# A hybrid encoder trunk: the correction of a softmax's 1/sum written into the sum's PSUM bank, and another order of matmuls in the values' projection

## The chip, the cores and the metric

One core of a Trainium2 chip. The metric is the device time of one execution in microseconds (us), the median over several executions. The engines are PE (TensorE, with its weight loads, PEld), DVE (VectorE), ACT (ScalarE), POOL (GpSimd) and SP (SyncE, which issues the DMAs).

## The reference, cut to what matters

x is 1 x 1024 tokens x 1024 features, float32. Two layers, each with a mixer and a feed-forward part: layer 0 mixes with 8 heads of latent attention (MLA) and 8 heads of stick-breaking attention, layer 1 with 16 heads of attention in chunks over a band of 9 chunks of 64 tokens.

```python
# MLA, per block of 128 queries
p_a = jax.nn.softmax(jnp.where(chunk_ok, s_a, -jnp.inf), axis=-1)
outs_a.append(jnp.einsum('bhqk,bkhd->bqhd', p_a.astype(v_a.dtype), v_a[:, :kend]))
# band
p = jax.nn.softmax(jnp.where(valid[None, :, None, None, :], scores, -jnp.inf), axis=-1).astype(v.dtype)
parts = [jnp.einsum('bnhqk,bnkhd->bnqhd', p[..., i * CHUNK:(i + 1) * CHUNK], v_p[:, i:i + n_chunks])
         for i in range(LEFT_CHUNKS + 1)]
o = functools.reduce(jnp.add, parts)
```

In both softmaxes the kernel divides at the end: it sums the exponentials, multiplies the unnormalised result with 1/sum, and so needs one reciprocal of a 128 x 512 tile for each pair of heads and each half of the tokens.

## The kernel before, in words

Activations lie transposed, 128 features (or two heads of 64) on the partitions and 512 tokens (a half, `hf`) along the free dimension. A float32 product is made of three matmuls in the rounded type fp32r: high by high, high by low, low by high (`mm3`, L277 to L282, so a product shows as L280, L281, L282). A tile and its rest are made by `split`: a cast (L243 on ACT, or L245 on DVE and POOL) and a subtraction (L248, "rest").

A framework's scheduler orders the instructions of each engine by priority and its own cost estimates, gives out the buffers of each named pool and sets the semaphores; only the feed-forward parts keep the order of the program. PSUM has three pools: `mm` (2 buffers of one bank, `bank`), for projections; `z` (2 buffers of two banks, `banks`, L199), for scores, maxima and sums; `o` (2 banks), for attention results. The SBUF tiles named `f` rotate through 3 buffers in mixer 0 and 2 in mixer 1.

Attention runs head pair by head pair, and in each the first half of the tokens before the second. `weave` (L785) mixes its steps with a filling generator: the projections of the next head pair, and at their end the values of a coming one. For the softmaxes each step has score matmuls (L1120 to L1122 in MLA, L1201 and L1202 in the band) into a `z` buffer, an addition of the bias on DVE in the band (L1203), an exponential on ACT, the running sum `esum` on POOL (L1072), and the product with the values (L831). A second set of score matmuls (L1049 in MLA, L1175 in the band) and reductions on DVE (L1051, L1178, result `m`) find the maxima for the coming half.

`soft_finish` (L1084) ends each half of a head pair; it runs 8 times in MLA and 16 times in the band. Two matmuls for each of the two heads add up `esum` over the partitions into `den`, one bank of a `z` buffer (L1088). ACT forms r = exp(-ln(den)) (L1090, L1091). DVE then corrects r by one Newton step: t = -den * r (L1092), r = (t + 2) * r (L1093); and L1094 forms the result from `o`, a PSUM bank, and r.

`values` (L798) projects the values of two head pairs, 256 columns. Four tiles of weights, quarters with two of the 8 features each, are loaded and split (`wh` by ACT, `wl` by DVE; four buffers of each, shared with the other projections). The stationary operand is a block of 128 tokens, the moving one 128 x 256 weights, so that one bank of 512 columns takes two token blocks; a call for one half fills two banks. It is called in the stick-breaking part for head pairs 0 and 1, ahead of the band's attention, and in the band for head pairs 0 to 5. Calls for MLA's own values have one block in a bank.

## Time and profile before

| | us |
|---|---|
| median of 3 executions | 2609.49 |
| lowest, highest | 2604.78, 2610.32 |
| the profiled execution | 2615.43 |
| its span in the profile | 2613.3 |

The stages in the profiled execution, with busy time of PE and DVE in us and the mean granted clock of PE:

| stage | from, to | PE | DVE | POOL | clock |
|---|---|---|---|---|---|
| opening: norm, first values and keys | 0, 70 | 53.3 | 45.0 | 24.0 | 0.95 |
| stick-breaking attention, MLA's projections | 70, 430 | 342.2 | 308.9 | 128.8 | 0.99 |
| MLA's attention | 430, 660 | 223.6 | 158.0 | 120.6 | 0.98 |
| feed-forward 0 | 660, 1310 | 639.7 | 469.1 | 7.2 | 1.00 |
| band: first values and projections | 1310, 1376 | 63.1 | 40.8 | 16.7 | 1.00 |
| band's attention | 1376, 1905 | 516.3 | 384.5 | 194.5 | 1.00 |
| feed-forward 1 | 1905, 2550 | 635.6 | 466.7 | 4.4 | 0.99 |
| final norm | 2550, 2613 | 47.8 | 38.6 | 26.6 | 0.93 |

A row of the timeline gives start and duration of one instruction, its engine, line, operation and tiles (out<-in), and in brackets how long the engine stood idle before it and which instruction's semaphore ended that. PE's durations overlap, since matmuls are pipelined; the step from start to start is the rate. Rows of groups give count, busy time, mean duration in ns and the idle time before the group's instructions. The releaser of a wait is inferred.

### The profile page before, as it was taken

What the parts mean: (1) busy time and instruction counts of PE and PEld (TensorE: products, weight loads), DVE (VectorE), ACT (ScalarE), POOL (GpSimd) and SP (SyncE); (2) the same over time, 40 slices, a digit from 0 to 9 for tenths busy, and PEclk for the clock granted to TensorE, in tenths of its full rate; (3) what the DMA queues carried; (4) which work ended last, traced back from release to release, by engine and by line L of the source; (5) the groups of instructions that cost most, each with busy time, mean ns of one, the idle gap of its engine ahead of it and who ended that gap; (6) DMA issues with size and microseconds to landing.
All of it is one profiled execution on the core that took longest, in us unless ns stands there. A gap on an engine that the chain in (4) does not pass through costs nothing.

```text
span 2613.3 us, 33627 instructions
## 1 busy us (share of the span) xinstructions
PE 2521.6 (96%) x11758; PEld 1941.0 (74%) x11758; DVE 1911.5 (73%) x3072; ACT 1169.0 (45%) x2028; POOL 522.9 (20%) x489
## 2 busy tenths in 40 slices
PE   7999999999999999999999999999999999999997
PEld 6766765557778888888787666676777888888876
DVE  6888887775787666777666777777778766667776
ACT  4677676454454334432253333334444443443324
POOL 3333324663000000000021333335400000000004
PEclk9999998999999999999999999999999999999999
DMA  4221100125434344476642222222552434447661
GB/s 137 61 63 53 53 17 29 35 64 159 163 99 161 110 140 142 149 258 216 206 160 67 73 78 80 73 69 89 172 166 96 162 109 141 145 140 260 213 213 69
DMA packets 179433, 319.70 MB, mean 122 GB/s; under 512 B 20545, under 2 KB 36801, under 8 KB 179265
## 3 DMA queue, kind: packets, MB, share of 16 engines
q1 hardware_dynamic: 179264, 317.56, 36.8%
q8 instruction: 93, 1.52, 0.3%
q14 instruction: 76, 0.61, 0.1%
HBM read 222.58 MB, written 84.41 MB: 117 GB/s over the span
## 4 chain that ended last, share of the span: by engine, by line
PE 68%; DVE 12%; DMA 2%; issue 2%; ACT 2%; SPq 0%; DVEq 0%; ACTq 0%
PE z L74 24%; PE mm L74 12%; PE o L74 6%; PE mm L280 5%; PE mm L281 5%; PE mm L282 5%; PE o L831 3%; DVE u L74 2%; DVE f L1093 2%; PE z L1201 1%; PE z L1175 1%; PE z L1202 1%; DVE u L303 1%; DMA wr<-in_w_down 1%; PE z L1088 1%
## 5 line engine op out<-in xcount | busy, mean ns | idle before, releaser
L74 PE MATMUL z<-u,vh 128*128 128x512 f32 x976 | 304.6, 393 | 7.2 <-DVE u L74 7.2
L74 PE MATMUL z<-u,wh 128*128 128x512 f32 x976 | 302.3, 390 | 6.5 <-DVE u L74 6.5
L280 PE MATMUL mm<-u,wh 128*128 128x512 f32 x720 | 291.7, 405 | 2.4 <-DVE u L710 1.1
L281 PE MATMUL mm<-u,wh 128*128 128x512 f32 x720 | 284.4, 395 | 1.4 <-DVE u L248 1.4
L248 POOL TENSOR_TENSOR wl<-wr,wh 128x512 fp32r<-128x512 f32 (+2 forms) x95 | 123.6, 1308 | 802.4 <-ACT wh L243 733.6
L282 PE MATMUL mm<-u,wl 128*128 128x512 f32 x720 | 283.8, 394 | 0.0
L74 PE MATMUL mm<-u,wh 128*128 128x512 f32 x720 | 224.6, 393 | 3.8 <-ACT wh L74 3.8
L74 PEld LDWEIGHTS z<-u,vh 128*128 128x128 f32 x976 | 184.5, 189 | 48.1 <-ACT u L74 8.8
L74 PEld LDWEIGHTS z<-u,wh 128*128 128x128 f32 x976 | 183.1, 188 | 47.4 <-DVE u L74 9.4
L74 PE MATMUL z<-u,vl 128*128 128x512 f32 x488 | 191.1, 392 | 0.0
L74 PE MATMUL z<-u,wl 128*128 128x512 f32 x488 | 190.0, 389 | 0.0
L280 PEld LDWEIGHTS mm<-u,wh 128*128 128x128 f32 x720 | 135.6, 188 | 62.2 <-issue 33.1
L831 PE MATMUL o<-a,u 128*64 128x512 f32 (+3 forms) x768 | 172.4, 485 | 0.3 <-ACT a L1204 0.3
L74 PEld LDWEIGHTS mm<-u,wh 128*128 128x128 f32 x720 | 135.5, 189 | 34.9 <-ACT wh L74 5.7
L281 PEld LDWEIGHTS mm<-u,wh 128*128 128x128 f32 x720 | 135.8, 189 | 32.5 <-issue 8.3
L282 PEld LDWEIGHTS mm<-u,wl 128*128 128x128 f32 x720 | 135.5, 188 | 32.3 <-issue 3.6
L74 PE MATMUL mm<-u,vh 128*128 128x512 f32 x496 | 152.7, 389 | 0.0
L248 POOL TENSOR_TENSOR u<-wr,u 128x512 fp32r<-128x512 f32 x8 | 10.9, 1373 | 671.7 <-ACT u L243 671.7
L74 PE MATMUL mm<-u,wl 128*128 128x512 f32 x360 | 141.2, 392 | 0.7 <-DVE wl L74 0.5
L1204 ACT ACTIVATE a<-a 128x1024 f32<-128x1024 f32 (+3 forms) x96 | 70.6, 738 | 155.3 <-DVE a L1203 155.0
L1072 POOL TENSOR_TENSOR b<-b,a 128x512 f32<-128x512 f32 (+3 forms) x80 | 110.6, 1382 | 135.8 <-ACT a L1204 117.4
L1203 DVE TENSOR_TENSOR a<-z,bias 128x1024 f32<-128x1024 f32 (+3 forms) x96 | 78.7, 823 | 79.5 <-PE z L1202 65.6
(248 smaller groups left out, 5983.1 us busy)
## 6 DMA issues: line engine op xcount, KB each, us to landing
u<-f_t SPq DMA_DIRECT2D x144, 256.0 KB, 5.2
vr<-in_w_up SPq DMA_DIRECT2D x88, 256.0 KB, 4.4
wr<-in_w_gate SPq DMA_DIRECT2D x88, 256.0 KB, 3.5
f_t<-x SPq DMA_DIRECT2D x72, 256.0 KB, 2.0
wr<-in_w_out SPq DMA_DIRECT2D x64, 256.0 KB, 3.0
f_t<-e SPq DMA_DIRECT2D x54, 256.0 KB, 3.6
ld<-f SPq DMA_DIRECT2D x54, 256.0 KB, 5.2
h<-u SPq DMA_DIRECT2D x48, 256.0 KB, 2.5
```

The source lines that it names most:

```text
L74: return lambda *a, **k: self.tc.keep_in_program_order(f(*a, **k))
L248: self.eng(eng).tensor_tensor(lo, src, hi.bitcast(F32), ALU.subtract)
L280: mm(out, wh, xh, start=first, stop=False, skip_group_check=onto)
L281: mm(out, wh, xl, start=False, stop=False, skip_group_check=onto)
L282: mm(out, wl, xh, start=False, stop=last, skip_group_check=onto)
L303: self.eng(eng).tensor_tensor(acc, acc, sq, ALU.add)
L831: self.nc.tensor.matmul(o[rh, cs], vt[j // 4][:, j % 4, rh], w[:, e, cs], start=first, stop=last)
L1072: self.eng("dve" if dest[2] else "pool").tensor_tensor(st["esum"][:, :, cs], old[:, :, cs], ex[:, :, cs], ALU.add)
L1088: nc.tensor.matmul(den[64 * e:64 * e + 64, :], self.ones[:, 0:64], esum[:, e, :], start=True, stop=True)
L1093: nc.vector.scalar_tensor_tensor(r, t, 2.0, r, ALU.add, ALU.mult)
L1203: nc.vector.tensor_tensor(ex[:, :, cs], z[:, :, cs], tk[:, :, xs], ALU.add)
L1204: nc.scalar.activation(ex[:, :, cs], ex[:, :, cs], AF.Exp)
```

## The change

In `soft_finish` the tile t is gone: L1092 writes -den * r over den in its PSUM bank, and L1093 reads that bank and r. The `z` buffer that holds den is in use until L1093 now. In `values` the two loops are exchanged: for each feature k the three matmuls of the first block, then the three of the second; the first matmul of the bank alone clears it (start), and the last one ends it.

```diff
-            for b in range(per):
-                hf, r = divmod(b0 + b, 4)
-                ts = slice(r * P, (r + 1) * P)
-                for k in range(nk):
+            for k in range(nk):
+                for b in range(per):
+                    hf, r = divmod(b0 + b, 4)
+                    ts = slice(r * P, (r + 1) * P)
                     wh, wl = ws[k // kper].at(k % kper * ncol, ncol)
                     self.mm3(ps[:, b * ncol:(b + 1) * ncol], u[hf][0][k][:, ts], u[hf][1][k][:, ts],
-                             wh, wl, k == 0, k == nk - 1)
+                             wh, wl, k == 0 and b == 0, k == nk - 1 and b == per - 1)
                     yield 3 * MM_US * ncol / HALF
...
-        r, t, ot = self.tmp("f"), self.tmp("f"), self.tmp("f")
+        r, ot = self.tmp("f"), self.tmp("f")
         nc.scalar.activation(r, den, AF.Ln)
         nc.scalar.activation(r, r, AF.Exp, scale=-1.0)
-        nc.vector.scalar_tensor_tensor(t, den, -1.0, r, ALU.mult, ALU.mult)
-        nc.vector.scalar_tensor_tensor(r, t, 2.0, r, ALU.add, ALU.mult)
+        nc.vector.scalar_tensor_tensor(den, den, -1.0, r, ALU.mult, ALU.mult)
+        nc.vector.scalar_tensor_tensor(r, den, 2.0, r, ALU.add, ALU.mult)
```

The scheduler keeps the feed-forward parts as they were. Names carry running numbers, which are smaller after the change since a tile is missing.

DVE at the end of the band's first head pair, second half (f are r, t and ot, z den or scores, bias the bias, mm a projection). Before:

```order
L1203 TENSOR_TENSOR a_12987<-z_12988,bias_12786 128x2x384
L1092 SCALAR_TENSOR_TENSOR f_12979<-z_12975,f_12978 128x512
L1139 SCALAR_TENSOR_TENSOR t_13012<-mm_12951,u_11665 128x512
L1093 SCALAR_TENSOR_TENSOR f_12978<-f_12979,f_12978 128x512
L1178 ISA z_12999,m_12998<-z_12999,bias_12781 128x512
L1178 ISA m_12998 128x1
L1094 TENSOR_TENSOR f_12980<-o_12669,f_12978 128x512
L1178 ISA z_12999,m_12998<-z_12999,bias_12781 128x512
```

And after the change:

```order
L1203 TENSOR_TENSOR a_12977<-z_12978,bias_12777 128x2x384
L1092 SCALAR_TENSOR_TENSOR z_12966<-z_12966,f_12969 128x512
L1139 SCALAR_TENSOR_TENSOR t_13002<-mm_12942,u_11657 128x512
L1093 SCALAR_TENSOR_TENSOR f_12969<-z_12966,f_12969 128x512
L1178 ISA z_12989,m_12988<-z_12989,bias_12772 128x512
L1178 ISA m_12988 128x1
L1094 TENSOR_TENSOR f_12970<-o_12660,f_12969 128x512
L1178 ISA z_12989,m_12988<-z_12989,bias_12772 128x512
```

The order of DVE is the same there; den's buffer (z_12975, now z_12966) is read two instructions later than before.

PE at the same place, behind the sum's matmuls (L1088): score matmuls for the maxima (L1175) between those of a projection (L280 to L282). Before:

```order
L282 MATMUL mm_13024<-u_11698,wl_12942 128x512
L1175 MATMUL z_12999<-u_12641,u_12568 128x512
L1175 MATMUL z_12999<-u_12647,u_12573 128x512
L1175 MATMUL z_13004<-u_12692,u_12568 128x128
L1175 MATMUL z_13004<-u_12698,u_12573 128x128
L280 MATMUL mm_13024<-u_11725,wh_12941 128x512
L281 MATMUL mm_13024<-u_11726,wh_12941 128x512
```

After:

```order
L282 MATMUL mm_13014<-u_11690,wl_12933 128x512
L1175 MATMUL z_12989<-u_12632,u_12560 128x512
L1175 MATMUL z_12989<-u_12638,u_12565 128x512
L280 MATMUL mm_13014<-u_11717,wh_12932 128x512
L281 MATMUL mm_13014<-u_11718,wh_12932 128x512
L282 MATMUL mm_13014<-u_11717,wl_12933 128x512
L280 MATMUL mm_13014<-u_11745,wh_12932 128x512
L281 MATMUL mm_13014<-u_11746,wh_12932 128x512
L282 MATMUL mm_13014<-u_11745,wl_12933 128x512
L1175 MATMUL z_12994<-u_12683,u_12560 128x128
L1175 MATMUL z_12994<-u_12689,u_12565 128x128
```

The second pair of L1175 (z_13004, now z_12994) stands six matmuls of the projection later.

PE in the values' projection of the same head pair's first half (mm is the bank, wh and wl weights, u activations), around the first use of the fourth quarter of the weights (wh_12724 and wl_12725, now wh_12715 and wl_12716). Before, where the bank's first matmul stands 23 rows ahead of that use:

```order
L280 MATMUL mm_12728<-wh_12718,u_11597 128x256
L281 MATMUL mm_12728<-wl_12719,u_11597 128x256
L282 MATMUL mm_12728<-wh_12718,u_11598 128x256
L280 MATMUL mm_12728<-wh_12724,u_11625 128x256
L281 MATMUL mm_12728<-wl_12725,u_11625 128x256
L282 MATMUL mm_12728<-wh_12724,u_11626 128x256
```

After, where it stands 48 rows ahead:

```order
L280 MATMUL mm_12719<-wh_12709,u_11589 128x256
L281 MATMUL mm_12719<-wl_12710,u_11589 128x256
L282 MATMUL mm_12719<-wh_12709,u_11590 128x256
L280 MATMUL mm_12719<-wh_12715,u_11617 128x256
L281 MATMUL mm_12719<-wl_12716,u_11617 128x256
L282 MATMUL mm_12719<-wh_12715,u_11618 128x256
```

Of these rows 18 were matmuls of the values and are 36 now; the others are attention.

DVE in the stick-breaking attention of the first head pair, where the next projection's weights are cast (L245, wh) and their rests formed (L248, wl), between the steps of the attention (L897, L900, L924, L927). Before:

```order
L897 TENSOR_SCALAR a_1334<-z_1329 128x1024
L924 TENSOR_TENSOR b_999<-z_1318,b_999 1x1024
L900 TENSOR_TENSOR b_1269<-b_1269,a_1268 128x1024
L927 TENSOR_TENSOR a_1170<-a_1170,z_1318 128x1024
L248 TENSOR_TENSOR c_1275<-b_1269,c_1274 128x512
L900 TENSOR_TENSOR b_1335<-b_1335,a_1334 128x1024
L245 CAST wh_1417<-wr_1415 128x512
L245 CAST wh_1423<-wr_1421 128x512
L248 TENSOR_TENSOR wl_1418<-wr_1415,wh_1417 128x512
```

After:

```order
L245 CAST wh_1417<-wr_1415 128x512
L248 TENSOR_TENSOR wl_1418<-wr_1415,wh_1417 128x512
L897 TENSOR_SCALAR a_1334<-z_1329 128x1024
L924 TENSOR_TENSOR b_999<-z_1318,b_999 1x1024
L900 TENSOR_TENSOR b_1269<-b_1269,a_1268 128x1024
L927 TENSOR_TENSOR a_1170<-a_1170,z_1318 128x1024
L248 TENSOR_TENSOR c_1275<-b_1269,c_1274 128x512
L900 TENSOR_TENSOR b_1335<-b_1335,a_1334 128x1024
L245 CAST wh_1423<-wr_1421 128x512
```

The first cast and its rest stand ahead of L897 and six more instructions now.

## Rows read from the trace of the kernel before

**Rows 1.** The page: busy time, and the chain that ended last, by line.
```profile
PE 2521.6 (96%) x11758; PEld 1941.0 (74%) x11758; DVE 1911.5 (73%) x3072; ACT 1169.0 (45%) x2028; POOL 522.9 (20%) x489
...
PE z L74 24%; PE mm L74 12%; PE o L74 6%; PE mm L280 5%; PE mm L281 5%; PE mm L282 5%; PE o L831 3%; DVE u L74 2%; DVE f L1093 2%; PE z L1201 1%; PE z L1175 1%; PE z L1202 1%; DVE u L303 1%; DMA wr<-in_w_down 1%; PE z L1088 1%
```

**Rows 2.** Groups of DVE by line: count | busy us, mean ns | idle.
```profile
L1093 DVE SCALAR_TENSOR_TENSOR f<-f,f 128x512 f32<-128x512 f32 x24 | 45.0, 1877 | 0.6
```

**Rows 3.** Timeline of DVE and POOL, end of a first half in the band.
```profile
1436.95 2.83 DVE L1093 SCALAR_TENSOR_TENSOR f<-f,f 128x512 f32<-128x512 f32 x1
1439.81 0.69 DVE L248 TENSOR_TENSOR u<-t,u 64x512 fp32r<-64x512 f32 x1
...
1436.85 2.38 POOL L1072 TENSOR_TENSOR b<-a,a 128x1024 f32<-128x1024 f32 x1 [3.75 <-ACT a L1204]
```

**Rows 4.** Timeline of DVE, POOL and PE, end of a second half in the band.
```profile
1473.87 2.30 DVE L1093 SCALAR_TENSOR_TENSOR f<-f,f 128x512 f32<-128x512 f32 x1
1476.10 0.68 DVE L1178 CUSTOM_DVE_ANT_0 z<-z,bias 128x512 f32<-128x512 f32 x1
...
1473.78 1.84 POOL L1072 TENSOR_TENSOR b<-a,a 128x768 f32<-128x768 f32 x1 [5.99 <-ACT a L1204]
...
1478.10 0.39 PE L1201 MATMUL z<-u,u 128*128 128x256 f32 x1 [1.14 <-DVE m L1178]
```

**Rows 5.** Groups of PE by line, 1376 to 1905 us, idle time in the last column.
```profile
L1201 PE MATMUL z<-u,u 128*128 128x512 f32 (+3 forms) x192 | 66.4, 357 | 5.7 <-DVE m L1178 5.7
L281 PE MATMUL mm<-wl,u 128*128 128x256 f32 x202 | 57.7, 286 | 4.3 <-DVE wl L248 4.3
```

**Rows 6.** Timeline of PE and DVE, values' projection in a first half.
```profile
1445.27 0.28 PE L282 MATMUL mm<-wh,u 128*128 128x256 f32 x1
1445.38 0.28 PE L280 MATMUL mm<-wh,u 128*128 128x256 f32 x1
1446.15 0.39 PE L281 MATMUL mm<-wl,u 128*128 128x256 f32 x1 [0.49 <-DVE wl L248]
...
1444.10 2.00 DVE L248 TENSOR_TENSOR wl<-wr,wh 128x512 fp32r<-128x512 f32 x1 [0.82 <-ACT wh L243]
```

**Rows 7.** Timeline of PE, two starts of a projection in stick-breaking attention.
```profile
139.23 0.27 PE L895 MATMUL z<-u,u 128*128 128x128 f32 x1
140.03 0.51 PE L280 MATMUL mm<-u,wh 128*128 128x512 f32 x1 [0.53 <-DVE wh L245]
...
213.00 0.50 PE L280 MATMUL mm<-u,wh 128*128 128x512 f32 x1 [0.53 <-DVE wh L245]
```

**Rows 8.** Timeline of DVE, POOL and PE, a softmax's end in MLA.
```profile
511.60 0.69 DVE L1092 SCALAR_TENSOR_TENSOR f<-z,f 128x512 f32<-128x512 f32 x1
512.33 4.13 DVE L1093 SCALAR_TENSOR_TENSOR f<-f,f 128x512 f32<-128x512 f32 x1
...
510.99 1.18 POOL L248 TENSOR_TENSOR wl<-wr,wh 128x256 fp32r<-128x256 f32 x1
...
513.55 5.13 POOL L1072 TENSOR_TENSOR b<-b,a 128x1024 f32<-128x1024 f32 x2
...
517.57 0.44 PE L1120 MATMUL z<-u,u 104*128 104x384 f32 x1 [2.37 <-DVE m L1051]
```

**Rows 9.** Groups of PE by line, 430 to 660 us.
```profile
L1120 PE MATMUL z<-u,u 100*128 100x512 f32 (+4 forms) x96 | 36.9, 385 | 5.0 <-DVE m L1051 3.7 <-DVE f L1092 0.7 <-DVE u L1035 0.6
```

**Rows 10.** One stretch: busy us of PE, PEld, DVE, ACT, POOL; clock; DMA.
```profile
518.30:521.70 3.40, 3.40 (x11) 1.57 (x10) 0.69 (x1) 0.81 (x1) 1.84 (x2) 0.51 0.41 125
```

**Rows 11.** Who waited for L1092: us, times.
```profile
  PEld z L1120: 3.2, 3
  PEld z L1175: 1.8, 6
```

**Rows 12.** Timeline of PE, values in the opening stage, a change of region.
```profile
33.29 0.28 PE L282 MATMUL z<-wh,u 128*128 128x256 f32 x1
33.41 0.28 PE L280 MATMUL z<-wh,u 128*128 128x256 f32 x1
```

## The prediction, made before the changed kernel was run

> **What bounds the kernel now.** I read the page first: TensorE (PE) is busy 96% of the span, and the chain that ended last goes through matmuls for 68%; the only line of the softmax's end on it is L1093, a VectorE (DVE) instruction with 2% of the chain [rows 1]. So an edit pays only where PE stands still, and I then looked for those places. The groups by line say that L1093 is odd: 24 instructions of 128x512 take 45.0 us, 1.88 on average [rows 2]. Undisturbed ones of that size take 0.69, like L1092 in [rows 8] and L248 in [rows 3]. So 45.0 - 24 x 0.69 = 28.4 us of DVE time are something else. The timeline shows what: each long L1093 runs beside a GpSimd (POOL) addition and ends 0.5 to 0.6 us after it. At 1436.95 it takes 2.83 us, beside a POOL L1072 of 1436.85 to 1439.23 [rows 3]; at 1473.87 it takes 2.30, beside one of 1473.78 to 1475.62 [rows 4]; at 512.33 it takes 4.13, beside L1072's of 513.55 and after [rows 8]. Most of the 28.4 us is hidden. PE stood still for it in these places:
> - second halves of the band's head pairs (5 of them, period 62.3 us): L1178 starts only at 1476.10, and PE's L1201 waits at 1478.10 for that line's maxima; 5.7 us of idle time in all five [rows 4, 5];
> [...]
>
> The other part of the change concerns two more waits: in the first halves PE's L281 stands at 1446.15 before the fourth quarter of the values' weights, whose rest (L248, wl) DVE finishes at 1446.10; six places, 4.3 us of idle time [rows 5, 6]; and in the stick-breaking part a projection waits at 140.03 for its weights (L245) [rows 7].
>
> **The change, part by part.** Values first. A bank has 2 blocks x 8 features x 3 = 48 matmuls, 0.12 us apart (1445.27 to 1445.38) [rows 6]. Before, the fourth quarter is first needed after 18 of them, after the change after 36: 18 x 0.12 = 2.1 us more, and the order shows seven more rows of attention matmuls in between as well. The late rest of 1446.10 is then wanted at 1445.5 + 2.1 = 1447.6 or later: that wait goes, with 1.5 us to spare. A start-to-start step shows what it costs: 0.77 us (1445.38 to 1446.15) for a usual 0.12, so 0.65 against 0.49 shown as idle; the 4.3 us of idle are therefore 4.3 to 5.7 us. **I take 5.0.** In the second bank each quarter is done 18 matmuls earlier too, so weight buffers come free earlier; the order shows DVE's first cast of the next projection (L245 with its L248) moved ahead of two L900 and an L897. PE's start at 140.03 comes 0.80 after the matmul before it, which is of 128 columns and needs some 0.1: 0.7 us lost, and the same at 213.00 in the next head pair: **1.4 us**. The moved casts cost DVE nothing new, they are the same instructions; what they push back by some 1.1 us is L897, and I keep 0 to 1 us for that in the range. Switching between two regions of a bank costs nothing: the values of the opening stage already change region every three matmuls (33.29 to 33.41 is such a change), at the same 0.12 [rows 12]. The DMAs of these weights only move by places; nothing of the sum hangs on them.
>
> The softmax's end. L1092 now reads and writes PSUM, which the trace has no STT for; the nearest row is L1178, PSUM to PSUM with one SBUF input, 0.68 us [rows 4]. L1093 gets one PSUM and one SBUF input instead of two SBUF ones. Of that kind are L1092, which took 0.69 at 511.60 although POOL's L248 ran until 512.17 [rows 8], and L1178. I therefore take L1093 at 0.69 in all places; the other end is the 1.88 it has now, that is no gain.
>
> [...]
>
> What it gives, place by place:
> - first halves: 1439.81 is an L248 with two SBUF inputs, so it takes over the wait for POOL until 1439.23; DVE gains the 0.69 only, and PE does not wait there. **0**;
> - second halves: behind L1093 stand L1178, L1094, L1178, each with one SBUF input, so all move 2.30 - 0.69 = 1.6 us ahead, more than the 1.14 that PE waits: **5.7**;
> - MLA: the waits for L1051, **3.7**, go, as 4.13 and its like become 0.69. [...]
>
> What it costs: the bank of the sum (one of two in the pool z, through which all scores go) is free after L1093, no longer after L1092. PE's weight loads waited for L1092 in 9 of the 24 places [rows 11]. Three are L1120 in MLA, where L1093 stands right behind: 3 x 0.69 = **2.1**. Six are L1175 (0.30 us each); there the order moves that pair of matmuls six matmuls of 512 columns back, each two steps of the 0.12 us of 256: 6 x 0.24 = 1.4 us, while L1093 ends at 1473.87 + 0.68 = 1474.55, 1.2 after L1092 now: nothing new, and the 0.30 that may go are not counted. In the 15 other places nobody waits for this bank now; a new wait there is between 0 and 0.69 us, 10.4 in all. I take **2**, since the bank's next user is several matmuls away in the places I read.
>
> Sum: 5.0 + 1.4 + 5.7 + 3.7 + 1.7 - 2.1 - 2 = 13.4 us. The profiled execution took 2615.4 (its span 2613.3), 5.9 over the median of the runs, 2609.5. So 2602 on the profile's scale and 2609.5 - 13.4 = **2596** on the runs'.
>
> **Rivals.** *The block stays with DVE* (chance 0.15). POOL's additions hold up whatever DVE instruction is there, L1178 or L1093 from PSUM too. Against it: L1092 beside POOL at 511.60, and L1178 at 0.68. For it: no row shows an STT whose PSUM input has just been written by the instruction before. Then 5.0 + 1.4 remain less 2 of bank waits: 2605, within what a measurement tells from no change, which is 0.2% (5.2 us) here.
>
> *The stall moves on* (0.17). With PE ahead by 1.1 to 1.5 us in each half, it meets the next thing that is just in time: the maxima of the next half, exponentials of ACT, POOL's sums before L1088. PE has slack nowhere (96%), DVE does. If half of the terms from the softmax's end (11.1) is given back so: 5.5 less, 2601.5.
>
> *The bank held longer decides* (0.10), the slower side. In all 24 places the next score matmul waits for L1093: 24 x 0.69 = 16.6 us, and in the five second halves L1139 and in six first halves L248 stands between the two, 11 x 0.68 = 7.5 more, 24 in all. The gains ahead of the costs are 17.5 (5.0 + 1.4 + 5.7 + 3.7 + 1.7), so it decides from 17.5 / 24 = 0.73 us of new wait in each place; in full it gives 2609.5 + 24.1 - 17.5 = 2616. For it: 9 of 24 places have a waiter today. Against it: PE's own rows between, as in the moved L1175.
>
> **How the numbers follow.** The forecast has 0.58, its own range 2590 to 2605: at the low end 5.7 + 1.4 + 5.7 + 3.7 + 1.7, and 5 x 0.30 for L1175, = 19.7 without any cost, 2589.8; at the high end the values at 4.3 and 10.4 of bank waits, 13.4 - 0.7 - 8.4 = 4.3, 2605.2. "The stall moves on" lies inside. Together 0.75; with a part of the blocked case, 8 in 10 are held from 2588 to 2608. Faster by over 0.2% means under 2604.3: nearly all of the forecast and of the moved stall, 0.73. Within 0.2%: the blocked case and what is left, 0.17. Slower: 0.10, the bank.
>
> **What would show it.** L1093 at about 0.7 us in all 24 places, total near 16.5 instead of 45.0; L1201's and L1051's idle sums near 0; no waits for wl at L281 of 256 columns; no low clock at 518. Bank waits would stand as idle time of L1175, L1120 or L1201 ended by DVE's L1093, and over 0.7 us in most places proves the third rival. If L1093 is still over 2 us beside POOL, the first holds. If L1093 is short and other PE waits of a microsecond are new, the second.

## The result, and the profile after

Six executions of each kernel: 2608.55 us before (2604.51 to 2610.34), **2593.66 us after** (2590.0 to 2597.0); the ratio is 0.9945, with a 95% interval of 0.9931 to 0.9959. That is 14.9 us less; forecast were 13.4 us, and 2596 us. The profiled execution of after has a span of 2589.5 us, 23.8 less than the one of before, so some 9 us between these two traces are not the change's. The stages show where they lie. Each stage below is taken from the start of one matmul to that of another (the first L894, the first L1120, the first L74 behind it, the last L74 ahead of the band, the first L1201, the first L74 behind it, the last L74), in us:

| stage | before | after |
|---|---|---|
| opening | 72.9 | 69.1 |
| stick-breaking attention, MLA's projections | 356.6 | 354.3 |
| MLA's attention | 229.7 | 229.5 |
| feed-forward 0 | 645.3 | 644.5 |
| band: first values and projections | 103.6 | 103.3 |
| band's attention | 494.8 | 481.7 |
| feed-forward 1 | 646.9 | 643.6 |
| final norm | 63.5 | 63.5 |

The opening took from 69.1 to 73.2 us in the fourteen traces of this study, though no kernel changes it, and feed-forward 1 from 641.9 to 646.9, each with a varying number of stretches at a granted clock of 0.50 for 1.00: in the opening one of 6.8 us before and none after, in feed-forward 1 three of 3.4 us each before and one after. Those are most of the 9 us. The stages that the change touches give 2.3 + 0.2 + 13.1 = 15.6 us, which agrees with the 14.9 of the medians.

The page of after, busy time and the chain that ended last [rows 1]:

```profile
PE 2513.1 (97%) x11758; PEld 1938.4 (75%) x11758; DVE 1890.9 (73%) x3072; ACT 1168.4 (45%) x2028; POOL 517.0 (20%) x489
...
PE z L74 24%; PE mm L74 12%; PE o L74 6%; PE mm L280 6%; PE mm L281 6%; PE mm L282 6%; PE o L831 4%; DVE u L74 2%; PE z L1201 2%; PE z L1175 1%; PE z L1202 1%; PE z L1120 1%; DVE u L303 1%; PE z L1088 1%; PE z L1121 1%
```

L1093 has left the chain. Groups of DVE of after, count | busy us, mean ns | idle [rows 2]:

```profile
L1092 DVE SCALAR_TENSOR_TENSOR z<-z,f 128x512 f32<-128x512 f32 x24 | 16.7, 695 | 8.4 <-ACT f L1091 8.2
L1093 DVE SCALAR_TENSOR_TENSOR f<-z,f 128x512 f32<-128x512 f32 x24 | 16.5, 688 | 0.5
```

All 24 of L1093 together went from 45.0 to 16.5 us, and L1092, which writes PSUM now, is 0.01 us longer than the 0.69 it had. The timeline of after at the ends of the first half and of the second half of the band's first head pair, DVE and POOL, and PE in the second [rows 3, 4]:

```profile
1429.63 0.69 DVE L1093 SCALAR_TENSOR_TENSOR f<-z,f 128x512 f32<-128x512 f32 x1
1430.35 2.10 DVE L248 TENSOR_TENSOR u<-t,u 64x512 fp32r<-64x512 f32 x1
...
1429.52 2.38 POOL L1072 TENSOR_TENSOR b<-a,a 128x1024 f32<-128x1024 f32 x1 [3.81 <-ACT a L1204]
...
1465.78 0.68 DVE L1093 SCALAR_TENSOR_TENSOR f<-z,f 128x512 f32<-128x512 f32 x1
1466.38 0.69 DVE L1178 CUSTOM_DVE_ANT_0 z<-z,bias 128x512 f32<-128x512 f32 x1
...
1465.69 1.85 POOL L1072 TENSOR_TENSOR b<-a,a 128x768 f32<-128x768 f32 x1 [5.84 <-ACT a L1204]
...
1467.68 1.08 PE L831 MATMUL o<-a,u 128*64 128x512 f32 x4
1468.69 0.39 PE L1201 MATMUL z<-u,u 128*128 128x256 f32 x1
```

And the matmuls ahead of L1201 in the kernel before, whose own row stands in [rows 4]:

```profile
1475.88 1.08 PE L831 MATMUL o<-a,u 128*64 128x512 f32 x4
```

In the first half POOL's addition now holds up the next instruction with two SBUF inputs, L248, which went from 0.69 to 2.10 us; in the second half nothing is held up, and PE's L1201 starts without a wait: 1.01 us behind the first of the four L831, where before it was 1478.10 - 1475.88 = 2.22. Groups of PE of after in the band, with idle time [rows 5]:

```profile
L281 PE MATMUL mm<-wl,u 128*128 128x256 f32 x192 | 54.3, 283 | 0.0
L1201 PE MATMUL z<-u,u 128*128 128x512 f32 (+3 forms) x192 | 66.4, 357 | 0.0
L1175 PE MATMUL z<-u,u 128*128 128x128 f32 (+3 forms) x192 | 47.4, 331 | 0.8 <-DVE m L1178 0.5 <-DVE a L1203 0.2
```

The 4.3 us and 5.7 us of idle time are gone, and the matmuls of the values still follow one another at 0.12 us. Who waited for L1093, and so for the bank [rows 11 of L1092]:

```profile
  PEld z L1201: 4.1, 5
  PEld z L1049: 0.8, 1
```

Only weight loads did, while the matmuls ahead of them were still running. In MLA, groups of PE and two of its waits [rows 9]:

```profile
L280 PE MATMUL mm<-u,wh 128*128 128x512 f32 x114 | 46.8, 410 | 1.8 <-DVE c L989 1.8
L1120 PE MATMUL z<-u,u 100*128 100x512 f32 (+4 forms) x94 | 35.4, 376 | 0.9 <-ACT a L1123 0.7 <-DVE m L1051 0.2
...
542.48 0.47 PE L280 MATMUL mm<-u,wh 128*128 128x512 f32 x1 [1.80 <-DVE c L989]
...
579.44 0.65 PE L1088 MATMUL z<-b,ones 128*64 128x512 f32 x2 [1.47 <-DVE b L1072]
```

L1120's waits for L1051 fell from 3.7 to 0.2 us as forecast, but the stage took as long as before: the scheduler ordered it anew, and two waits of 1.80 and 1.47 us stand where before there were none.

### The profile page after: what moved, and what is told of

Read it like the earlier page. It is cut to its first block, busy times and chain, and to the rows that moved or that the text cites. A ratio compares the mean times of both kernels' runs of the same rounds, so it can differ in the third digit from the quotient of the medians.

```text
span 2589.5 us, 33647 instructions
## 1 busy us (share of the span) xinstructions
PE 2513.1 (97%) x11758; PEld 1938.4 (75%) x11758; DVE 1890.9 (73%) x3072; ACT 1168.4 (45%) x2028; POOL 517.0 (20%) x489
## 4 chain that ended last, share of the span: by engine, by line
PE 73%; DVE 8%; DMA 2%; ACT 1%; issue 1%; POOL 0%; DVEq 0%; SPq 0%; POOLq 0%; ACTq 0%
PE z L74 24%; PE mm L74 12%; PE o L74 6%; PE mm L280 6%; PE mm L281 6%; PE mm L282 6%; PE o L831 4%; DVE u L74 2%; PE z L1201 2%; PE z L1175 1%; PE z L1202 1%; PE z L1120 1%; DVE u L303 1%; PE z L1088 1%; PE z L1121 1%
## 5 line engine op out<-in xcount | busy, mean ns | idle before, releaser
L74 PE MATMUL z<-u,vh 128*128 128x512 f32 x976 | 304.0, 393 | 4.6 <-DVE u L74 4.6
L74 PE MATMUL z<-u,wh 128*128 128x512 f32 x976 | 302.2, 390 | 6.4 <-DVE u L74 6.4
L280 PE MATMUL mm<-u,wh 128*128 128x512 f32 x720 | 291.7, 405 | 2.9 <-DVE c L989 1.8
L248 POOL TENSOR_TENSOR wl<-wr,wh 128x512 fp32r<-128x512 f32 (+2 forms) x95 | 122.0, 1289 | 809.2 <-ACT wh L243 739.0
L282 PE MATMUL mm<-u,wl 128*128 128x512 f32 x720 | 282.9, 393 | 0.0
L74 PE MATMUL mm<-u,wh 128*128 128x512 f32 x720 | 223.4, 392 | 4.5 <-ACT wh L74 4.5
L74 PEld LDWEIGHTS z<-u,wh 128*128 128x128 f32 x976 | 183.2, 188 | 47.3 <-DVE u L74 9.5
L74 PEld LDWEIGHTS z<-u,vh 128*128 128x128 f32 x976 | 184.4, 189 | 45.4 <-ACT u L74 6.2
L74 PE MATMUL z<-u,vl 128*128 128x512 f32 x488 | 191.1, 392 | 0.0
L74 PE MATMUL z<-u,wl 128*128 128x512 f32 x488 | 189.9, 389 | 0.0
L280 PEld LDWEIGHTS mm<-u,wh 128*128 128x128 f32 x720 | 135.5, 188 | 64.8 <-issue 40.3
L831 PE MATMUL o<-a,u 128*64 128x512 f32 (+3 forms) x768 | 171.8, 483 | 0.2 <-ACT a L1204 0.2
L74 PEld LDWEIGHTS mm<-u,wh 128*128 128x128 f32 x720 | 134.7, 188 | 35.7 <-ACT wh L74 6.9
L282 PEld LDWEIGHTS mm<-u,wl 128*128 128x128 f32 x720 | 135.6, 188 | 29.2 <-issue 2.1
L74 PE MATMUL mm<-u,vh 128*128 128x512 f32 x496 | 152.7, 389 | 0.0
L248 POOL TENSOR_TENSOR u<-wr,u 128x512 fp32r<-128x512 f32 x8 | 10.9, 1374 | 668.6 <-ACT u L243 668.6
L74 PE MATMUL mm<-u,wl 128*128 128x512 f32 x360 | 140.8, 391 | 0.8 <-DVE wl L74 0.5
L1204 ACT ACTIVATE a<-a 128x1024 f32<-128x1024 f32 (+3 forms) x96 | 70.6, 738 | 144.6 <-DVE a L1203 144.4
L74 ACT CAST vh<-vr 128x512 fp32r<-128x512 f32 (+1 forms) x166 | 95.9, 577 | 80.2 <-DVE vr L74 31.2
L1203 DVE TENSOR_TENSOR a<-z,bias 128x1024 f32<-128x1024 f32 (+3 forms) x96 | 78.8, 823 | 70.1 <-PE z L1202 54.7
```

The lines of the kernel that those rows point to most:

```text
L74: return lambda *a, **k: self.tc.keep_in_program_order(f(*a, **k))
L248: self.eng(eng).tensor_tensor(lo, src, hi.bitcast(F32), ALU.subtract)
L280: mm(out, wh, xh, start=first, stop=False, skip_group_check=onto)
L282: mm(out, wl, xh, start=False, stop=last, skip_group_check=onto)
L831: self.nc.tensor.matmul(o[rh, cs], vt[j // 4][:, j % 4, rh], w[:, e, cs], start=first, stop=last)
L1203: nc.vector.tensor_tensor(ex[:, :, cs], z[:, :, cs], tk[:, :, xs], ALU.add)
```

## The experiments

The two parts can be made apart, so the first question was whether each gives what the prediction put down for it. The theory was the prediction's: PE's waits for late DVE results are what is gained, place by place. The rivals: the stalls move on, or the bank held longer takes the gain back.

### Each part alone

The values' part alone:

```diff
-            for b in range(per):
-                ...
-                for k in range(nk):
+            for k in range(nk):
+                for b in range(per):
```

> Only the values' part of the change: the loops over features and blocks exchanged, the softmax's end as before. My theory: the six waits of L281 for wl (4.3 us idle, 5.2 us by start-to-start steps) and the two waits for the weights' cast in stick-breaking attention (1.4 us) go, the five of L1201 for L1178 (5.7 us idle) stay: 6 to 7 us less than before, a ratio of 0.9975. Rival, the stall moves on: PE meets the next late operand, 3 us less or nothing. Second rival: the gain of the second halves of the band is owed to the moved L1175 pair, which this part brings, and not to L1093: then 11 to 12 us less here, and L1201's idle time near 0.

2603.14 us, ratio 0.9978 (0.9969 to 0.9987): by the ratio 5.7 us less. But it is not where I had put it. Groups of PE in the band, and one of its new waits:

```profile
L1201 PE MATMUL z<-u,u 128*128 128x512 f32 (+3 forms) x192 | 66.4, 357 | 9.4 <-DVE m L1178 5.7 <-DVE a L1203 3.8
L281 PE MATMUL mm<-wl,u 128*128 128x256 f32 x192 | 54.3, 283 | 0.0
...
1504.28 0.44 PE L1201 MATMUL z<-u,u 128*128 128x384 f32 x1 [0.65 <-DVE a L1203]
```

The waits for wl are gone (4.3 to 0.0), and six waits for L1203 of 3.8 us in all have come, a few matmuls later in the same halves. The band's attention took 493.1 us for 494.8: 1.7 us, not 5. Stick-breaking attention took 353.9 for 356.6: 2.7 us, not 1.4. L1201's wait for L1178 stayed at 5.7. That says nothing on the second rival: in this kernel's trace the L1175 pair stands where it stood before; it moves in the kernel with the softmax's end alone, so the expectation had it in the wrong part.

The softmax's end alone:

```diff
-        r, t, ot = self.tmp("f"), self.tmp("f"), self.tmp("f")
+        r, ot = self.tmp("f"), self.tmp("f")
...
-        nc.vector.scalar_tensor_tensor(t, den, -1.0, r, ALU.mult, ALU.mult)
-        nc.vector.scalar_tensor_tensor(r, t, 2.0, r, ALU.add, ALU.mult)
+        nc.vector.scalar_tensor_tensor(den, den, -1.0, r, ALU.mult, ALU.mult)
+        nc.vector.scalar_tensor_tensor(r, den, 2.0, r, ALU.add, ALU.mult)
```

> Only the softmax's end: t in den's PSUM bank, values' loops as before. My theory: L1093 takes 0.69 us in all 24 places; L1201's 5.7 us of idle time go, and some of the L1175 waits turn up, since the pair isn't moved back here and waits for L1093 now (five times up to 1 us); the scheduler orders the last two head pairs of MLA anew with new waits of its own, which take back what MLA gains. 6 to 9 us less than before, ratio 0.997. Rival, the bank held longer decides: L1175 waits of 1.2 us or more in five places and others besides, 0 to 3 us less only, and all the rest of the changed kernel's gain is owed to the two parts together. Second rival, the parts simply add up: 14.9 less what the values' part alone gives.

2596.55 us, ratio 0.9953 (0.994 to 0.9965): 12.3 us less by the ratio, more than I expected. The ratios of the parts come to 5.7 + 12.3 = 18.0 us, for 14.3 with both, but each has an interval of 2 to 4 us either way, so this difference is not clear of the noise; the stages below are the better account. The band's attention took 483.1 us, 11.7 less. Its groups of PE:

```profile
L1201 PE MATMUL z<-u,u 128*128 128x512 f32 (+3 forms) x192 | 66.4, 357 | 0.0
L281 PE MATMUL mm<-wl,u 128*128 128x256 f32 x192 | 54.8, 285 | 0.1
```

The waits for wl are gone here as well, but for steps of 0.30 us instead of 0.12 in five of the six places, without the other order of the values' matmuls. How far PE's L1201 is ahead of the same matmul in the kernel before, counted from the stage's first, shows what each place gives:

| PE's lead grows by, us | values' part | softmax's end | both |
|---|---|---|---|
| in each of the six first halves | 0.3 | 0.7 | 0.7 in the first, then 1.0 |
| in each of the five second halves | 0 | 1.4 | 1.4 |
| band's attention in all | 1.7 | 11.7 | 13.1 |

So in the band the parts do add up (1.7 + 11.7 = 13.4, for 13.1), and in stick-breaking attention too (2.7 - 0.3, for 2.3). What overlaps is the waits for wl: either part ends them, but only the softmax's end turns most of them into time. The timelines of DVE, ACT and POOL behind L1093 in a first half show the connection; first the kernel before, then this one:

```profile
1441.73 0.95 DVE L1203 TENSOR_TENSOR a<-z,bias 128x768 f32<-128x768 f32 x1
...
1442.72 0.84 ACT L1204 ACTIVATE a<-a 128x768 f32<-128x768 f32 x1 [4.08 <-DVE a L1203]
1443.47 0.60 ACT L243 CAST wh<-wr 128x512 fp32r<-128x512 f32 x1
...
1443.70 1.84 POOL L1072 TENSOR_TENSOR b<-b,a 128x768 f32<-128x768 f32 x1 [4.47 <-ACT a L1204]
```

```profile
1433.39 0.69 DVE L1093 SCALAR_TENSOR_TENSOR f<-z,f 128x512 f32<-128x512 f32 x1
1434.11 2.10 DVE L248 TENSOR_TENSOR u<-t,u 64x512 fp32r<-64x512 f32 x1
...
1437.44 0.95 DVE L1203 TENSOR_TENSOR a<-z,bias 128x768 f32<-128x768 f32 x1
1439.81 1.98 DVE L248 TENSOR_TENSOR wl<-wr,wh 128x512 fp32r<-128x512 f32 x1 [0.82 <-ACT wh L243]
...
1438.43 0.84 ACT L1204 ACTIVATE a<-a 128x768 f32<-128x768 f32 x1 [3.37 <-DVE a L1203]
1439.18 0.60 ACT L243 CAST wh<-wr 128x512 fp32r<-128x512 f32 x1
```

The late rest wl waits for ACT's cast of wh; that cast stands on ACT behind the exponential L1204; the exponential waits for DVE's L1203; and L1203 stands on DVE behind L1093. From L1093's start to the rest of wl it was 1444.10 - 1436.95 = 7.15 us and is 1439.81 - 1433.39 = 6.42: 0.73 us, just what L1093 and the L248 behind it got shorter together (2.83 + 0.69 for 0.69 + 2.10). The idle time at the wl waits was 0.49 us in the first place and 0.76 on average in the five others. So the wait for wl and the wait for L1203 hang on one late L1093, and whoever defers the use of wl alone meets the late L1203 next. The chain has a second hold-up that neither part touches: the rest of wl itself has two SBUF inputs and runs beside POOL's addition of 1443.70, which makes 2.00 us of it before the change and 1.98 here, where another L248 of 128x512 takes 0.68 at 1441.13. What ending that would give, no run shows.

### The two halves of the values' part

A call fills two banks. Exchanging the loops in one of them separates the later need of the fourth quarter (first bank) from the earlier release of the weights' buffers (second bank).

```diff
+            turn = b0 == 4 * hfs[0]
+            for k, b in [(k, b) for k in range(nk) for b in range(per)] if turn else \
+                    [(k, b) for b in range(per) for k in range(nk)]:
```

> Of the values' part only the first bank of each call: features outside, blocks inside there; the second bank as before. No engine's instructions change their order otherwise, only which of the values' matmuls comes when. It tests the later need alone. My theory: as with the whole values' part alone the six waits for wl in the band go and come back as waits of L1201 for L1203 (3.8 us of idle time there), so the band's attention takes 493 to 495 us, and stick-breaking attention stays at 356.6: 0 to 2 us less than before. As the prediction had it: 5 us less.

2603.43 us, ratio 0.9982 (0.9973 to 0.9991); with `!=` for `==`, the second bank alone:

> Of the values' part only the second bank of each call: it tests the earlier release of the weights' buffers alone. My theory: DVE's casts of the next projection move ahead in stick-breaking attention, whose 356.6 us become 354.2 (the two waits for L245, and what follows them); the waits for wl in the band stay: 2 to 3 us less than before. Rival: the casts only push L897 and L900 back, nothing gained: 0.

2605.27 us, ratio 0.9987 (0.9979 to 0.9996). Groups of PE in the band, first of the first bank alone, then of the second (both kernels' lines from `values` on stand one further down: L1202 is L1201 of before):

```profile
L1202 PE MATMUL z<-u,u 128*128 128x512 f32 (+3 forms) x192 | 66.4, 357 | 9.4 <-DVE m L1179 5.7 <-DVE a L1204 3.7
L281 PE MATMUL mm<-wl,u 128*128 128x256 f32 x195 | 55.2, 283 | 0.0
```

```profile
L1202 PE MATMUL z<-u,u 128*128 128x512 f32 (+3 forms) x192 | 66.4, 357 | 5.7 <-DVE m L1179 5.7
L281 PE MATMUL mm<-wl,u 128*128 128x256 f32 x193 | 55.2, 286 | 4.3 <-DVE wl L248 4.3
```

| us | before | first bank | second bank | both (values' part) |
|---|---|---|---|---|
| stick-breaking attention | 356.6 | 357.0 | 353.8 | 353.9 |
| band's attention | 494.8 | 493.3 | 494.6 | 493.1 |

The later need moves the waits in the band and gives 1.5 us there; the earlier release of buffers gives 2.8 us in stick-breaking attention and nothing in the band. By the ratios the second bank's kernel is 3.4 us faster than before, about what these stages say, and the first bank's 4.7, some 3 more than its one trace shows; where those 3 us lie stays open, near the edge of the interval as they are.

The gain in stick-breaking attention is not the waits for the casts, though. PE's idle time there is 16.4 us before and 16.2 in the changed kernel: the 1.06 us at L280 go, and waits of L916 for L927 come in the same two places (0.75 and 0.52 us). What changed is the products with the values, L831, at these places; here the first, before and then after the change:

```profile
140.71 1.07 PE L831 MATMUL o<-a,u 128*64 128x512 f32 x2
...
142.83 1.07 PE L831 MATMUL o<-a,u 128*64 128x512 f32 x2
```

```profile
137.12 1.08 PE L831 MATMUL o<-a,u 128*64 128x512 f32 x4
```

The four belong to two heads. In a row they start in pairs, two of them 0.01 us apart, and the next matmul starts 1.0 us behind the first. Before the change the scheduler had put the projection's matmuls between the heads; two alone start 0.48 us apart and take the same 1.0 us, so each such place costs 1.0 us, 2.0 in the two. Counted from start to start, without its waits, L831 takes 42.3 us in this stage before, with the softmax's end alone and with the first bank alone, and 40.2 with the second bank and in the changed kernel. Up to 311 us into the stage the lead is 2.3 us in all kernels that exchange the second bank; what the two parts' kernels have beyond that is a shorter stretch at the clock of 0.50 (6.8 us for 10.2).

### What the bank costs

The third rival priced the bank of the sum, held longer. A small DVE instruction that reads den behind L1094 keeps it longer in the changed kernel. The expectation put that at 0.8 us; in the trace the new instruction ends 0.9 to 3.9 us behind the one that last read den, 2.2 on average, since other DVE work stands between:

```diff
         nc.vector.tensor_tensor(ot, o, r, ALU.mult)
+        nc.vector.scalar_tensor_tensor(self.junk, den[:, 0:1], 1.0, ot[:, 0:1], ALU.mult, ALU.mult)
```

> The changed kernel, and den's bank held still longer: behind L1094 a DVE instruction of one column reads den and the result, so the bank comes free some 0.8 us later in each of the 24 places. 24 x 0.1 us of DVE are new. If the bank is what nobody waits for (my theory after the first four runs: no wait of PE on L1093 is left in the changed kernel's trace, only 4.1 us of weight loads), the band's 529 us grow by less than 2 us and the whole by 0 to 4. If a bank held longer costs PE its length (the third rival of the prediction), 24 x 0.8 = 19 us more than the changed kernel.

2598.37 us, ratio 0.9957 (0.9943 to 0.9971): 4.7 us more than the changed kernel's 2593.66 by the medians, 3 by the ratios, whose intervals overlap. The band's attention took 486.8 us for 481.7, 5.1 more, where I had expected under 2. In its trace PE waits five times for L1203 again (its L1205), which has slipped back a little, with a step of 0.59 us each for 0.32 in the changed kernel:

```profile
1505.31 0.44 PE L1203 MATMUL z<-u,u 128*128 128x384 f32 x1 [0.21 <-DVE a L1205]
```

These are 1.4 of the 5.1 us. The rest comes with the scheduler's order for the longer hold. In the second halves it puts score matmuls for the maxima between the products of the two heads, which stood together in the changed kernel; that one first, then this one (L832 is L831):

```profile
1472.05 0.87 PE L831 MATMUL o<-a,u 128*64 128x384 f32 x4
```

```profile
1472.97 0.86 PE L832 MATMUL o<-a,u 128*64 128x384 f32 x2
...
1474.19 0.86 PE L832 MATMUL o<-a,u 128*64 128x384 f32 x2
```

The four took 0.79 us to the next matmul, and the two and two take 0.79 each. Without its waits this line takes 73.7 us in the band for 69.4. So holding the bank longer costs here mostly by what the scheduler does, with 0.35 us of PE waiting for the new instruction, far from a bank that costs its length in every place, which would be 24 x 2.2 = 53 us. In the kernel before, with t in SBUF, den held until behind L1093:

```diff
         nc.vector.scalar_tensor_tensor(r, t, 2.0, r, ALU.add, ALU.mult)
+        nc.vector.scalar_tensor_tensor(self.junk, den[:, 0:1], 1.0, r[:, 0:1], ALU.mult, ALU.mult)
```

> The kernel before with the cost of the softmax's part and without its gain: t stays in SBUF, L1093 has two SBUF inputs, and behind it a DVE instruction of one column reads den, so that the bank is held until then. The scheduler then orders the work much as for the part of the softmax alone. My theory: L1093 is as long as before (45 us in all), and the bank held for up to 4 us more costs; the band loses 1 us in each half at which L1175 or L1201 waits for the bank, 2 to 10 us more than before in all. If instead the order that comes with a longer hold were what gave the gain, this kernel would be 5 us or more faster than before, with L1093 as long as ever.

2611.38 us, ratio 1.0011 (1.0001 to 1.002): slower, as expected, at the low end of the 2 to 10 us. DVE's long instruction and PE behind it, in a second half (lines one or two further down: L1094 is L1093, L1177 is L1175):

```profile
1473.72 2.31 DVE L1094 SCALAR_TENSOR_TENSOR f<-f,f 128x512 f32<-128x512 f32 x1
...
1476.56 0.15 DVE L1095 SCALAR_TENSOR_TENSOR junk<-z,f 128x1 f32<-128x1 f32 x1
...
1476.77 0.33 PE L1177 MATMUL z<-u,u 128*128 128x128 f32 x1 [1.29 <-DVE junk L1095]
```

Here the bank is what PE waits for, 1.29 us at this place and likewise in the four other second halves. This is the third rival's mechanism, with the contention left in; but these waits, 6.5 us in all, stand where the kernel before has its 5.7 us for L1178, and the band's attention is only 0.9 us longer (495.7 for 494.8). The L1175 pair stands further back here too, and nothing is gained: an order of that kind does not gain without the short L1093. A kernel with a short L1093 and the pair in its old place was not made.

### MLA's share

The changed kernel with MLA's 8 places as before (t in an SBUF tile there):

```diff
+        t = den if self.inplace else self.tmp("f")
...
-        nc.vector.scalar_tensor_tensor(den, den, -1.0, r, ALU.mult, ALU.mult)
-        nc.vector.scalar_tensor_tensor(r, den, 2.0, r, ALU.add, ALU.mult)
+        nc.vector.scalar_tensor_tensor(t, den, -1.0, r, ALU.mult, ALU.mult)
+        nc.vector.scalar_tensor_tensor(r, t, 2.0, r, ALU.add, ALU.mult)
```

> The changed kernel, but in MLA's 8 places t goes to an SBUF tile as before; in the band's 16 places and in the values' projection as changed. My theory from the trace of the changed kernel: MLA's stage takes as long as before, since waits of 2.0, 1.6 and 0.5 us (L280 for L989, L1088 for L1072, L1120) stand where 3.7 us of waits for L1051 went; so this kernel is as fast as the changed one within 2 us (14.9 us less than before, ratio 0.994 to 0.995). Rival, the terms as I had predicted them (MLA worth 3.7 + 1.7 - 2.1 = 3.3 us): 3 us slower than the changed kernel, and the clock falls again behind the wait of 2.4 us.

2592.03 us, ratio 0.9936 (0.9922 to 0.9949). Once more, beside the changed kernel on one chip:

> The kernel with MLA's 8 places as before once more, beside the changed kernel on the same chip, since it came out at 0.9936 of before where the changed one had 0.9945. My theory: MLA's part of the change is worth nothing, 0 to 2 us faster than the changed kernel. The prediction's: 3 us slower than it.

> The changed kernel once more, on the same chip as the three others of this group. 0.9945 of before, between 0.993 and 0.996.

2592.0 (0.993 to 0.9957) against 2594.86 us (0.9935 to 0.996). And with only the three places of MLA as before from which its order changes (first halves of head pairs 1 to 3):

```diff
-(o_d[hf], p, p == 3)
+(o_d[hf], p, p == 3, (hf, p) not in ((0, 1), (0, 2), (0, 3)))
```

> The changed kernel, but in MLA's first halves of head pairs 1, 2 and 3 t goes to an SBUF tile as before; those are the three places from which the scheduler's order changes in MLA. All other 21 places in place. My theory: MLA's stage keeps the order of before and loses only the wait of 0.9 us at the first head pair (L1120 for L1051), so it takes 228.5 to 229.5 us without a low clock in it differing; the kernel is 0 to 2 us faster than the changed one. Rival, the order doesn't matter: as the changed kernel, within 1 us, or slower by the 2.4 us wait that stays at head pair 1.

2593.19 us, ratio 0.9943 (0.993 to 0.9955). The intervals of these kernels overlap, so none can be called faster than the changed one; what is shown is that MLA's 8 places are not worth the 3.3 us of the prediction. MLA's stage took 227.3 and 229.4 us without them, 227.8 with five of them, 229.5 and 230.8 with all, and 230.6 in the kernel with the softmax's part alone.

The clock explains part of that spread. The granted clock is at the lower level, 0.50, for 3.4 us of this stage in the traces of 227.3 and 227.8 us and for 6.5 to 6.8 in the four others, where the stage took 229.4 without MLA's places and 229.5 to 230.8 with them. One stretch each, right behind PE's wait of 2.37 us for L1051 in the first kernel without MLA's places, and from 545.3 us in the second trace of the changed kernel, behind its wait of 1.80 us for L989 (busy us of PE, PEld, DVE, ACT, POOL; clock; DMA):

```profile
515.50:519.00 3.50, 3.50 (x22) 2.31 (x22) 0.71 (x2) 1.12 (x2) 2.29 (x2) 1.00 0.47 150
```

```profile
545.30:548.70 3.40, 3.40 (x9) 2.75 (x9) 2.48 (x4) 0.62 (x1) 0.85 (x1) 0.50 0.22 75
```

Of the seven traces that have the 2.37 us wait, the clock fell to the lower level behind it in five ([rows 10] is one) and not in two. In one of the five it stayed there for 13.7 us, with the second bank alone, and the stage took 234.3 us. In the changed kernel that wait is gone, and the clock fell behind the new one of 1.80 us in one trace of two; it did so as well in both other traces with that wait (the softmax's end alone, and the last kernel below).

### The same step elsewhere

In the rotation of MLA's queries, L990 adds two SBUF tiles, one of which L989 has just formed from a projection's PSUM bank:

```diff
-        nc.vector.tensor_tensor(b[64:96, :], ps[96:128, :], cs[96:128, :], ALU.mult)
-        nc.vector.tensor_tensor(t[64:96, :], t[64:96, :], b[64:96, :], ALU.add)
+        nc.vector.tensor_tensor(ps[64:96, :], ps[96:128, :], cs[96:128, :], ALU.mult)
+        nc.vector.tensor_tensor(t[64:96, :], t[64:96, :], ps[64:96, :], ALU.add)
```

> The changed kernel, and the same step once more in MLA's rotation: L989 writes its product over ps in the projection's PSUM bank and L990 adds it from there, with one SBUF input instead of two; the tile b is gone, and a bank of the pool mm is held until L990 instead of L989. L990 took 2.31 us beside POOL in the trace of before. My theory: L990 at 0.69 in all places, DVE in MLA some 10 us less busy; PE's waits for L989 and L1051 that are left (1.8 + 0.9 + 0.2 + 0.2 us) partly go: 0 to 3 us faster than the changed kernel. Rival: the projection's bank, one of two, is held longer and the projections wait for it: 1 to 4 us slower. Second rival: the new order decides, either way, by up to 3 us, with L990 short all the same.

2596.59 us, ratio 0.9953 (0.9941 to 0.9966): 2.9 us above the changed kernel's median, with overlapping intervals. L990 did become short, 8.2 us for 12 where the changed kernel has 12.3, and PE now waits for it (a group of DVE, a wait of PE):

```profile
L990 DVE TENSOR_TENSOR c<-c,mm 32x512 f32<-32x512 f32 x12 | 8.2, 685 | 0.4
...
375.96 0.47 PE L280 MATMUL mm<-u,wh 128*128 128x512 f32 x1 [0.81 <-DVE f L990]
```

That is not shown to be the cost: the two such waits in stick-breaking attention are 1.9 us, where the changed kernel has one of 3.5 us for L989. What grew there is PE's wait for another DVE line, L303 (1.3 to 4.7 us); PE's idle time rose by about 2 us, as the stage did (356.3 for 354.3). So it looks like the second rival, the new order.

In stick-breaking attention L900 takes the maximum of two SBUF tiles; one of them is the scores, cut at 88:

```diff
-            nc.vector.tensor_tensor(t[:, :, cs], t[:, :, cs], zc[:, :, cs], ALU.max)
+            nc.vector.scalar_tensor_tensor(t[:, :, cs], z[:, :, cs], ZMAX, t[:, :, cs], ALU.min, ALU.max)
```

> The changed kernel, and the same step in stick-breaking attention: L900 takes its second operand from the scores' PSUM bank, max(t, min(z, 88)), and so has one SBUF input instead of two; the bank is held until then, behind two exponentials and logarithms of ACT. L900 took 1.23 us without POOL beside it and 2.31 with (128x1024). If the contention on L900 is what stick-breaking attention waits for, 3 us less or more. My theory: every step holds its buffer of the pool z, one of two, for some 3 us more there, and PE's next scores (L894), which wait for L897 today, wait for L900: of some 36 steps, 1 to 3 us each, 30 to 100 us more than the changed kernel. L900 itself is 1.2 us in all places.

2615.21 us, ratio 1.0025 (1.0015 to 1.0034): some 20 us more than the changed kernel, less than the 30 to 100 that I expected, in the direction expected. Stick-breaking attention took 373.6 us for 354.3. L900 gained 2.3 us in all (48.2 to 45.9), and PE waits more in each of its groups there:

```profile
L900 DVE SCALAR_TENSOR_TENSOR b<-z,b 128x1024 f32<-128x1024 f32 (+3 forms) x48 | 45.9, 956 | 10.5 <-ACT b L899 9.7
...
L894 PE MATMUL z<-u,u 128*128 128x512 f32 (+3 forms) x94 | 33.3, 362 | 3.4 <-DVE a L927 2.7 <-DVE b L900 0.5
...
L916 PE MATMUL z<-c,masks 128*128 128x512 f32 (+3 forms) x96 | 27.8, 367 | 6.1 <-DVE a L927 5.6 <-ACT c L904 0.5
```

The changed kernel has 1.3 and 1.8 us in the last two. These idle times account for some 6 of the 19 us. Another 6.7 lie in L831, which takes 46.9 us without its waits for 40.2: of its matmuls only 76 start beside another, for 92 in the changed kernel, since the scheduler's order has more heads' products apart. Where the remaining 6 lie stays open.

## Why the prediction was right, point by point

- **L1093.** Right: 0.69 us in all 24 places, with POOL beside it too; the first rival (the block stays with DVE) is out. As forecast, the block passes to L248 in the first halves (2.10 us).
- **Second halves, 5.7 us.** Right in place and mechanism: L1201's wait goes, 2.22 - 1.01 = 1.2 us, and PE's lead grows by 1.4 us in each, 7.0 in five. That L1093 does it, and not the L1175 pair that moves in the same kernels, is read from DVE's timeline; no run parts the two.
- **First halves, 0 us.** Of the step "DVE gains the 0.69 only, and PE does not wait there" the first half held (0.73 us) and the second failed. PE does wait there, two engines further: L1093, L1203, ACT's exponential, ACT's cast of wh, DVE's rest wl, PE. The softmax's end alone gives 0.7 us in each of the six, 4.4 in all.
- **Values in the band, 5.0 us.** The step "that wait goes, with 1.5 us to spare" is right for wl and failed for the gain: alone, this part gives 1.7 us there, as PE meets L1203 next, and beside the softmax's end 483.1 - 481.7 = 1.5. The two wrong terms cancel: with both parts the six first halves give 0.7 + 5 x 1.0, 5.8 us by the unrounded steps, where 0 + 5.0 had been booked.
- **Casts in stick-breaking attention, 1.4 us.** Right in place and in what starts it, the earlier release of the buffers (2.3 us measured); wrong in the mechanism. The waits for the casts only moved, and the time comes from the two heads' products, which stand together again. The size is luck.
- **MLA, 3.7 + 1.7 - 2.1 us.** Failed: 0.2 us measured. The waits went, and the order made from the new buffer times put new ones there. No run shows the 1.7 us put down for the clock, an estimate of mine booked as sure: the clock fell behind the old wait of 2.37 us in five traces of seven, and behind the new one of 1.80 us in three of four.
- **The bank, 2 us elsewhere.** Too much: no matmul of PE waits for L1093 in the changed kernel. Held 2.2 us longer still, the bank costs 5.1 us in the band, through the scheduler's order more than by waits.
- **The rivals.** "The stall moves on" happened in MLA, and to the values' part when alone. PE waits for the bank in earnest only where a long L1093 holds it, and there it costs 0.9 us in the band.

So the mechanism of the largest gain was right, and the total held better than its terms, in part by luck: MLA's 3.1 us too much stand against 2.4 too little in the band, 0.9 in stick-breaking attention and 2 of bank cost that did not come.

## What to carry to other kernels

Two late operands in one stretch can have one cause: before adding up the waits that two edits remove, follow each back over all engines, the in-order queues too, to where the chains meet; the experiment with each edit alone shows which of them gives the time, read stage by stage, since the whole times are too noisy for a few us. Handing an intermediate to PSUM was a cheap way out of a DVE instruction that POOL holds up (L1093, 45.0 to 16.5 us in 24 places), where the bank was held no longer than it took the next user to come; in the one place tried where the hold spans a wait for ACT, it cost 19 us and gave 2.3 of DVE's time. And where a scheduler orders the work, a changed buffer lifetime reorders a stage: look for its new waits before booking the old ones as gained, and for matmuls that ran side by side and were put apart, or together again, 1.0 us a place here: idle time does not show those.

## What the runs showed of the hardware

- A SCALAR_TENSOR_TENSOR (STT) on 128x512 that also writes to PSUM takes 0.695 us, 0.01 more than L1092 before with its SBUF output (0.686), and L1093 from PSUM takes 0.688, 0.01 more than its shortest run from two SBUF tiles (0.678).
- POOL's hold on DVE passes on: with L1093 at 0.69 us for 2.83 at the end of a first half in the band, the next instruction with two SBUF inputs, an L248, takes 2.10 us instead of 0.69 beside POOL's addition of 2.38.
- Two matmuls of 64 columns of weights each (`128*64`, L831), one of each of two heads, start 0.01 us apart when they follow one another, so four of them take 1.0 us with 512 columns moving; two of one head alone start 0.48 us apart and take 1.0 us as well.
- The granted clock fell to 0.50 behind the same wait of 2.37 us in five traces and not in two, for 3.4 us and once for 13.7; MLA's stage varied with it by 2 us, and once by 5.
- Accumulating two regions of a PSUM bank in turn, three matmuls each, leaves the matmuls of 256 columns at 0.12 us, as in one region.
